# The 24 gate columns of an input projection as four float32 column groups of the array

## The chip, the cores and the metric

The kernel runs on one core of a Trainium2 chip. The metric is the device time of one execution in microseconds, as the median of several runs. Five engines matter here, each with an instruction stream of its own that it works off in order: TensorE (PE in the profile; PEld is its loading of weights), VectorE (DVE), ScalarE (ACT), GpSimd (POOL) and SyncE (SP), which issues most of the transfers.

## What is computed

One step of a decoder layer with 512 prompt tokens and 8 samples of 8 tokens, 576 tokens in all, of width 2048, in float32. The input is normalised, projected by w_in, and split into the inputs of eight gated-delta heads and four mLSTM heads. After these come an output projection, a convolutional feed-forward block and a final norm. What the change touches is the beginning:

```
h = _rmsnorm(x, norm_mix_g)
proj = jnp.einsum('bld,de->ble', h, w_in)
dn_qkv, dn_z, dn_b, dn_a, ml_q, ml_k, ml_v, ml_o, ml_i, ml_f = jnp.split(proj, idx, axis=-1)
...
beta = jax.nn.sigmoid(dn_b)
g = -jnp.exp(dn_A_log) * jax.nn.softplus(dn_a + dn_dt_bias)
...
ig = ml_i + ml_i_bias
logf = jax.nn.log_sigmoid(ml_f + ml_f_bias)
```

The four small pieces dn_b, dn_a (8 columns each), ml_i and ml_f (4 each) are the 24 gate columns. All other pieces are multiples of 128 columns wide. The norm is a factor 1/sqrt(mean of squares + eps) for each token, times norm_mix_g for each of the 2048 rows of w_in.

## The kernel before

The data lie transposed: features on the 128 partitions, 576 tokens along the free dimension. The input x is thus 16 tiles of 128 x 576 (k = 0 to 15). A float32 product is made of three products of a faster type, float32r: every operand is split into a high and a low part (`split`, lines 118 to 121: ScalarE casts, which is line 120, VectorE subtracts, which is line 121), and `three` (line 194 on) multiplies high by high, high by low and low by high. Each is done for two halves of 288 tokens, so one k of one 128-column tile is six matmuls, all at line 198. I call this a step. `dense` (line 201) makes one 128-column tile of a product in 16 steps: 96 matmuls. Its weights come in units of 128 x 1024 (eight k), loaded by SP's queue up to three units ahead (`load_unit`, `unit`); a unit's raw buffer, its high and its low part have two buffers each.

`startup` (lines 333 to 367) issues the loads of x, and after x 1 and x 3 those of the first two units. For every k, ScalarE and VectorE make the high part ah and the low part al of x times norm_mix_g (lines 356 and 357). The factor 1/sqrt isn't in them; it is multiplied in when a tile leaves PSUM. For it ScalarE squares all x (line 363), GpSimd adds up those of odd k and VectorE those of even k (line 365), and VectorE adds the two (line 366).

`gates` (line 370) sets up constants and then makes the first tile of w_in. In this tile, the host has put the 24 gate columns at columns 0, 32, 64 and 96, and zeros elsewhere; it costs as much as any tile of 128. Its two halves stay in two PSUM tiles pr (there are four pr of one bank, and two pd of two banks for the dense tiles). `gate_rows` (line 398) is a job: a generator that is advanced by `tick` after each step, and whose `yield n` lets n steps pass. This is how all the small work is spread between the dense steps; TensorE's order is that in which the program issues. Here the job waits for 14 steps after its first tick, then sums the squares over the partitions with a matrix of ones (`rms_bc`, whose two products are at line 256), forms rstd on ScalarE and VectorE (lines 244 to 248), multiplies the gates by it (line 406), waits 6 steps, and then works out the gates' functions in some 40 instructions, chiefly on VectorE. After twice 30 more steps it transposes the results, and only then can the job of the first head begin.

`mixer` (line 284) goes through the heads: for each of the eight delta heads the tiles q, k, v and z; the first three go to `conv_in` (line 518), which takes a tile out of PSUM times rstd (lines 528 to 530), and convolves it. A dense tile needs one of the two pd, so its first step waits until the tile before the last has been taken out. A head's job `dn_head` starts when its four tiles are there and the head before the last is done, the first head's when the gates are done.

On ScalarE, VectorE, GpSimd and in SP's queue the order is planned at build time from priorities and estimated durations; `urgent` raises a priority. The chip then keeps to that order.

Of the kernel before, what the change touches and what calls it, by code (L numbers as in the profile page):

```python
# [43 lines left out]
# columns of the parameter array  # L44
G1, G2, G3, CW, DG, MG, FW, FBI, GB, AL, M0, NPAR = 0, 16, 32, 48, 144, 145, 153, 417, 505, 506, 507, 515
# columns of the constant array
C_ID, C_INC, C_LV, C_IS, C_BM, C_SG, C_BD, C_RB, C_M3, NCON = 0, 128, 256, 640, 704, 712, 713, 841, 849, 853

# order of the 128-column tiles of w_in
# [19 lines left out]
class Layer:  # L69
# [25 lines left out]
    def open(self, name, **k):  # L95
        """A pool that close() ends (last in, first out on its side of the memory)."""
        stack = ExitStack()
        self.stacks[name] = stack
        return stack.enter_context(self.tc.tile_pool(name=name, **k))
# [48 lines left out]
    def plain_weights(self):  # L148
        for name, n in (("w_in", NIN), ("w_out", KT), ("w_up", 2 * NPL - 2)):
            for t in range(n):  # L150
                for u in range(2):
                    yield self.I[name][t][u], False
# [4 lines left out]
    def down_weights(self, b):  # L157
        """The weights of the plain blocks from b on, up to the next one of seven products."""
# [24 lines left out]
    def later(self, n, out, in_):  # L183
        """A store, queued n steps from now."""
# [16 lines left out]
    def dense(self, outs=None):  # L201
        """One 128-column tile of a K=2048 product."""
# [17 lines left out]
    def dense_pair(self):  # L220
        """Two tiles by turns, so that the first rows of the input are done with early."""
# [28 lines left out]
    def sum_bc(self, ss):  # L250
        """Sums over partitions of ss [P, NT], on all partitions."""
# [32 lines left out]
    def mixer(self):  # L284
# [5 lines left out]
        for h in range(DNH):  # L290
            q, k, v = (self.conv_in(8 * i + h, self.dense()) for i in range(3))
# [40 lines left out]
    def startup(self):  # L332
# [14 lines left out]
        acts = [self.new_act(k) for k in reversed(range(KT))][::-1]  # L347
        for k in range(KT):
            x = self.r()
            xs.append(x)  # L350
            nc.sync.dma_start(out=x, in_=I["xT"][k])
            if k in (1, 3):
                self.load_unit()
# [13 lines left out]
        self.acc = acc  # L367

# [1 line left out]
    def gates(self):  # L370
# [23 lines left out]
        outs = [self.psr()[:, 0:HALF] for _ in range(2)]  # L394
        self.dense(outs)
        return self.spawn(self.gate_rows(outs))

    def gate_rows(self, outs):
        nc, I, O = self.nc, self.I, self.O
        V, A, Pl = nc.vector, nc.scalar, nc.gpsimd  # L400
        yield 14
        self.rms_bc(self.acc[0], self.rstd)
        gr = self.r()
        for hf in range(2):
            sl = slice(hf * HALF, (hf + 1) * HALF)
            V.tensor_tensor(out=gr[:, sl], in0=outs[hf], in1=self.rstd[:, sl], op=ALU.mult)
        yield 6
# [10 lines left out]
        # softplus(y) = max(y, 0) + log1p(exp(-|y|)), log1p(e) = 2 atanh(e / (2 + e))  # L418
# [40 lines left out]
        # gated delta rows: log decay G, -exp(G), exp(Glast - G)  # L459
# [6 lines left out]
        # mLSTM rows (partitions 64-67)  # L466
# [51 lines left out]
    def conv_in(self, t, pd):  # L518
        """Depthwise convolution and silu of a projected tile."""
# [27 lines left out]
    def decay(self, bc, cols):  # L547
        """exp(min(bc_i - col_j, 0)) on and above the diagonal, else 0 (rows j, columns i)."""
# [20 lines left out]
    def lasts_of(self, bc):  # L569
        """The columns of bc at each chunk's last token."""  # L570
# [6 lines left out]
    def dn_head(self, h, q, k, v, sz):  # L577
# [14 lines left out]
        # natural k, norms of k  # L592
# [30 lines left out]
        # U = c_j (k_j . k_i) E, KQ = (k_j . q_i) E  # L623
# [19 lines left out]
        # v / |k| natural  # L643
# [18 lines left out]
        # chunk by chunk over the prompt  # L662
# [32 lines left out]
        # output norm; the scale of q only enters through the guard  # L695
# [10 lines left out]
    def pack(self, t, n, tag, order):  # L706
        """32 rows of t at a time as three groups of rows, each the high or the low parts."""
# [934 lines left out]
```

## Time and profile before

| what | value |
|---|---|
| median of 3 runs | 2703.66 us (2702.69 to 2705.25) |
| the profiled execution's span | 2704.9 us, granted TensorE clock 0.995 |
| the gate tile, first matmul to the next tile's first | 10.69 to 25.98 us |
| sums of squares over the partitions, first matmul | 41.77 us |
| bytes moved | 304.02 MB, mean 112 GB/s |

The profile is of one execution. A row of a timeline gives start, duration, engine, line, operation, the tile written and those read, the shape and the number of instructions merged; in brackets stands how long the engine was idle before, and what ended that. A row of waits gives the total, the number and the longest wait. A window row gives for each engine the busy time and the number of instructions, then the granted clock of TensorE, the transfers' share and rate. Matmuls overlap in TensorE's pipeline, so the spacing of their starts counts, not the duration of one.

### The profile page before, as it was taken

The numbers are of one execution on the slowest core, as the hardware profiler recorded it, in microseconds if no ns is written. First come the engines' busy times: TensorE is split into PE (matmuls) and PEld (weight loads), VectorE is DVE, ScalarE is ACT, GpSimd is POOL, SyncE is SP. The second block draws the span as 40 slices with busy tenths as digits, with TensorE's granted clock in tenths as the row PEclk, the third lists the DMA queues.
The fourth block names the chain that finished last, engine by engine and source line by source line (L and its number), as shares of the span: only waits on it lengthen the run. The fifth ranks groups of instructions, "written<-read, shape, count | busy, mean of one in ns | idle before, by whom it ended". The sixth has DMA issues, their size and how long they took to land.

```text
span 2704.9 us, 48701 instructions
## 1 busy us (share of the span) xinstructions
PE 2661.1 (98%) x19895; PEld 2620.4 (97%) x19895; DVE 1992.4 (74%) x3346; ACT 1072.4 (40%) x1694; POOL 327.8 (12%) x637
## 2 busy tenths in 40 slices
PE   7999999999999999998999999999999999999998
PEld 7999999999999999998999999999999999999998
DVE  7887777764444332289888888888888888988656
ACT  5334344433333232254444444444444443434324
POOL 2223222222111001111000000000000100000001
PEclk9999999999999999999999999999999999999999
DMA  5222222223332334444333333333333373342333
GB/s 195 85 79 92 91 83 91 91 88 105 112 107 89 122 127 134 137 124 149 107 107 107 109 111 110 107 107 107 107 107 107 107 255 99 105 145 71 121 96 100
DMA packets 112233, 304.02 MB, mean 112 GB/s; under 512 B 21912, under 2 KB 28184, under 8 KB 112008
## 3 DMA queue, kind: packets, MB, share of 16 engines
q1 hardware_dynamic: 107896, 291.17, 34.1%
q0 software_dynamic: 1872, 7.37, 0.8%
q8 instruction: 156, 2.56, 0.4%
q10 hardware_dynamic: 2240, 2.36, 0.3%
q14 instruction: 69, 0.57, 0.1%
HBM read 264.79 MB, written 36.06 MB: 111 GB/s over the span
## 4 chain that ended last, share of the span: by engine, by line
PE 88%; DVE 4%; DMA 1%; ACT 1%; issue 1%; POOL 0%; SPq 0%; DVEq 0%
PE pd L198 35%; PE pr L1265 31%; PE pd L1265 12%; PE pr L198 3%; PE pr L1491 1%; DMA r<-hid 1%; PE pr L991 1%; DVE wl L121 1%; PE pr L737 1%; DVE bl L121 0%; POOL irk L613 0%; DVE r L1526 0%; PE pr L832 0%; PE pr L256 0%; ACT r L603 0%
## 5 line engine op out<-in xcount | busy, mean ns | idle before, releaser
L120 ACT CAST wh<-raw 128x1024 fp32r<-128x1024 f32 (+1 forms) x394 | 404.6, 1027 | 744.7 <-PE pd L198 410.6
L1265 PE MATMUL pr<-bh,wh 128*128 128x288 f32 x2120 | 627.5, 296 | 2.2 <-ACT bh L120 2.2
L1265 PE MATMUL pr<-bl,wh 128*128 128x288 f32 x2120 | 625.0, 295 | 0.7 <-DVE bl L121 0.6
L1265 PE MATMUL pr<-bh,wl 128*128 128x288 f32 x2120 | 625.2, 295 | 0.1
L121 DVE TENSOR_TENSOR wl<-raw,wh 128x1024 fp32r<-128x1024 f32 (+1 forms) x394 | 474.4, 1204 | 183.3 <-ACT wh L120 177.0
L198 PE MATMUL pd<-ah,wh 128*128 128x288 f32 x2496 | 558.4, 305 | 0.0
L198 PE MATMUL pd<-ah,wl 128*128 128x288 f32 x2496 | 534.4, 296 | 0.0
L198 PE MATMUL pd<-al,wh 128*128 128x288 f32 x2496 | 534.2, 296 | 0.0
L198 PEld LDWEIGHTS pd<-ah,wh 128*128 128x128 f32 x2496 | 401.0, 189 | 9.5 <-issue 2.9
L198 PEld LDWEIGHTS pd<-ah,wl 128*128 128x128 f32 x2496 | 401.9, 189 | 0.0
L1265 PEld LDWEIGHTS pr<-bl,wh 128*128 128x128 f32 x2120 | 400.7, 189 | 1.1 <-DVE bl L121 1.1
L198 PEld LDWEIGHTS pd<-al,wh 128*128 128x128 f32 x2496 | 401.8, 189 | 0.0
L1265 PEld LDWEIGHTS pr<-bh,wh 128*128 128x128 f32 x2120 | 399.3, 188 | 2.4 <-ACT bh L120 2.4
L1265 PEld LDWEIGHTS pr<-bh,wl 128*128 128x128 f32 x2120 | 399.5, 188 | 0.8 <-DVE wl L121 0.8
L120 ACT CAST wh<-s 128x1024 fp32r<-128x1024 f32 (+1 forms) x171 | 169.5, 991 | 362.9 <-DVE s L1230 139.3
L1265 PE MATMUL pd<-bh,wh 128*128 128x288 f32 x848 | 252.0, 297 | 5.6 <-ACT wh L120 5.6
L1265 PE MATMUL pd<-bh,wl 128*128 128x288 f32 x848 | 250.9, 296 | 1.7 <-DVE wl L121 1.7
L1265 PE MATMUL pd<-bl,wh 128*128 128x288 f32 x848 | 249.9, 295 | 0.0
L121 DVE TENSOR_TENSOR wl<-s,wh 128x1024 fp32r<-128x1024 f32 (+1 forms) x171 | 196.5, 1149 | 27.0 <-ACT wh L120 19.6
L1265 PEld LDWEIGHTS pd<-bh,wh 128*128 128x128 f32 x848 | 160.2, 189 | 6.1 <-ACT wh L120 6.1
L1265 PEld LDWEIGHTS pd<-bh,wl 128*128 128x128 f32 x848 | 160.7, 189 | 2.3 <-DVE wl L121 2.3
L1265 PEld LDWEIGHTS pd<-bl,wh 128*128 128x128 f32 x848 | 160.9, 190 | 0.0
(391 smaller groups left out, 3514.1 us busy)
## 6 DMA issues: line engine op xcount, KB each, us to landing
raw<-in_w_up SPq DMA_DIRECT2D x176, 512.0 KB
raw<-in_w_in SPq DMA_DIRECT2D x114, 512.0 KB
raw<-in_w_down SPq DMA_DIRECT2D x40, 512.0 KB
raw<-in_w_out SPq DMA_DIRECT2D x32, 512.0 KB
raw<-in_w_down SPq DMA_DIRECT2D x40, 384.0 KB
hid<-r SPq DMA_DIRECT2D x44, 288.0 KB
r<-hid SPq DMA_DIRECT2D x40, 288.0 KB
r<-in_xT SPq DMA_DIRECT2D x32, 288.0 KB
```

What stands on the lines that cost most here:

```text
L120: nc.scalar.copy(hi, src)
L121: nc.vector.tensor_tensor(out=lo, in0=src, in1=hi.bitcast(F32), op=ALU.subtract)
L198: mm(outs[hf], w, x[:, hf * HALF:(hf + 1) * HALF], start=first and i == 0, stop=last and i == 2)
L737: mm(pr[:, 16 * b:16 * b + 16], st[:, b], kqs[:, b].rearrange("p a w -> p (a w)"), start=True, stop=True)
L991: mm(pn[0:64, 0:257], self.qim[:, b], caug[b // 4][:, b % 4], start=b == 0, stop=False)
L1265: mm(out, w[:, ks], x[:, sl], start=k == 0 and i == 0, stop=k == nk - 1 and i == 2)
L1491: mm(pr[:, 0:n], w[:, ks], acts[kk][:, a * NT + sl.start:a * NT + sl.stop], start=kk == 0 and i == 0, stop=kk == FB - 1 and i == 2)
```

## The change

The gate tile leaves the dense product. In `startup`, four loads of 128 x 512 (four k of the first tile of w_in each) go to SP's queue ahead of x 0, 4, 8 and 12, and GpSimd picks out 32 columns for each k, eight from each of the four places, and multiplies them by norm_mix_g (`gate_weights`). The first two units, now of tile q, are loaded after x 3 and x 7. The job `gate_rows` multiplies these weights with the raw x in float32: 16 k times two halves, 32 matmuls of 32 columns. Matmul k + j writes to partitions 32 j to 32 j + 31 of PSUM, so four k run in four column groups of the array and give four partial sums. It does four k at its first tick, which comes ahead of tile q's first step, and four more after steps 4, 8 and 12. ScalarE copies the partial sums to SBUF. GpSimd builds a matrix pick from the identity, and after the sums of squares, 14 steps later, a float32 product with pick adds the four groups and spreads the gates to the partitions 0, 32, 64 and 96 where the rest expects them. The gates' functions follow 8 steps later instead of 6. Of head 0, the tiles q and k are both issued before the first of them is taken out of PSUM. Everything else is the same; comments were dropped.

```diff
-        for name, n in (("w_in", NIN), ("w_out", KT), ("w_up", 2 * NPL - 2)):
-            for t in range(n):
+        for name, t0, n in (("w_in", 1, NIN), ("w_out", 0, KT), ("w_up", 0, 2 * NPL - 2)):
+            for t in range(t0, n):
...
-            q, k, v = (self.conv_in(8 * i + h, self.dense()) for i in range(3))
+            if h == 0:
+                self.tick()
+                pds = [self.dense(), self.dense()]
+                q, k = (self.conv_in(8 * i, pd) for i, pd in enumerate(pds))
+            else:
+                q, k = (self.conv_in(8 * i + h, self.dense()) for i in range(2))
+            v = self.conv_in(16 + h, self.dense())
...
+        self.gw = self.r(shape=[P, KT, 32])
         for k in range(KT):
+            if k % 4 == 0:
+                self.gate_weights(k)
             x = self.r()
             xs.append(x)
             nc.sync.dma_start(out=x, in_=I["xT"][k])
-            if k in (1, 3):
+            if k in (3, 7):
                 self.load_unit()
...
-        self.acc = acc
+        self.acc, self.xs = acc, xs
+
+    def gate_weights(self, k):
+
+        raw = self.r(shape=[P, 4, 4, 32])
+        self.nc.sync.dma_start(out=raw, in_=self.I["w_in"][0][k // 8][:, k % 8 * P:(k % 8 + 4) * P].rearrange("p (k g w) -> p k g w", k=4, g=4))
+        shape = [P, 4, 4, 8]
+        self.nc.gpsimd.tensor_tensor(out=self.gw[:, k:k + 4].rearrange("p k (g w) -> p k g w", g=4), in0=raw[:, :, :, 0:8],
+                                     in1=self.par[:, G1 + k:G1 + k + 4].unsqueeze(2).unsqueeze(3).to_broadcast(shape), op=ALU.mult)
...
-        outs = [self.psr()[:, 0:HALF] for _ in range(2)]
-        self.dense(outs)
-        return self.spawn(self.gate_rows(outs))
-
-    def gate_rows(self, outs):
+        return self.spawn(self.gate_rows())
+
+    def gate_rows(self):
         nc, I, O = self.nc, self.I, self.O
         V, A, Pl = nc.vector, nc.scalar, nc.gpsimd
+        halves = [slice(hf * HALF, (hf + 1) * HALF) for hf in range(2)]
+
+        outs = [self.psr()[:, 0:HALF] for _ in range(2)]
+        for k in range(0, KT, 4):
+            for out, sl in zip(outs, halves):
+                for j in range(4):
+                    nc.tensor.matmul(out[32 * j:32 * j + 32], self.gw[:, k + j], self.xs[k + j][:, sl], start=k == 0, stop=k == KT - 4)
+            if k < KT - 4:
+                yield 4
+        parts = self.r()
+        for out, sl in zip(outs, halves):
+            A.copy(parts[:, sl], out)
+
+        pick = self.r(shape=[P, 4, 32])
+        Pl.memset(pick, 0.0)
+        for j in range(4):
+            s = slice(32 * j, 32 * j + 32)
+            Pl.tensor_copy(pick[s, :, 0:8], self.ident[s, s].rearrange("p (g w) -> p g w", g=4))
         yield 14
         self.rms_bc(self.acc[0], self.rstd)
         gr = self.r()
-        for hf in range(2):
-            sl = slice(hf * HALF, (hf + 1) * HALF)
-            V.tensor_tensor(out=gr[:, sl], in0=outs[hf], in1=self.rstd[:, sl], op=ALU.mult)
-        yield 6
+        for sl in halves:
+            pr = self.psr()[:, 0:HALF]
+            nc.tensor.matmul(pr, pick.rearrange("p g w -> p (g w)"), parts[:, sl], start=True, stop=True)
+            V.tensor_tensor(out=gr[:, sl], in0=pr, in1=self.rstd[:, sl], op=ALU.mult)
+        yield 8
```

## The prediction

> **What bounds the kernel now.** I read the page first, then the waits of the first 110 us, then the first 75 us instruction by instruction, because everything that the diff touches lies there.
>
> ```profile
> span 2704.9 us, 48701 instructions
> PE 2661.1 (98%) x19895; PEld 2620.4 (97%) x19895; DVE 1992.4 (74%) x3346; ACT 1072.4 (40%) x1694; POOL 327.8 (12%) x637
> PE 88%; DVE 4%; DMA 1%; ACT 1%; issue 1%; POOL 0%; SPq 0%; DVEq 0%
> ```
> ```profile
> PE pr L198 <- ACT wh L120: 10.7, 1, 10.7
> PE pr L256 <- DVE r L366: 3.6, 1, 3.6
> ```
>
> TensorE is the bound: 98% busy, 88% of the chain that ended last. Work taken off it shortens the kernel as long as no new wait appears. Two of its waits are in the start: 10.7 us until the first weights are cast, and 3.6 us at line 256, where it is ready to sum the squares over the partitions but the squares are not yet added up. Since TensorE works in program order, that second wait holds up all dense products behind it.
>
> ```profile
> 10.69 0.85 PE L198 MATMUL pr<-ah,wh 128*128 128x288 f32 x2 [10.69 <-ACT wh L120]
> 15.24 0.55 PEld L198 LDWEIGHTS pr<-ah,wh 128*128 128x128 f32 x2
> 25.98 0.43 PE L198 MATMUL pd<-ah,wh 128*128 128x288 f32 x2
> 37.71 0.43 PE L198 MATMUL pd<-ah,wl 128*128 128x288 f32 x2
> 41.77 1.24 PE L256 MATMUL pr<-r,ones 128*128 128x288 f32 x4 [3.63 <-DVE r L366]
> 42.63 0.73 PE L198 MATMUL pd<-ah,wh 128*128 128x288 f32 x2
> 46.49 0.42 PE L198 MATMUL pd<-ah,wl 128*128 128x288 f32 x2
> 57.96 0.43 PE L198 MATMUL pd<-ah,wh 128*128 128x288 f32 x2
> ```
>
> The gate tile takes 10.69 to 25.98, 15.3 us. Tile q of head 0 follows. Between 25.98 and 37.71 stand 15 steps of k, that is 45 pairs of matmuls, so a pair takes 11.73 / 44 = 0.267 us and a step of three pairs 0.80 us. After step 15 the sums are due, and TensorE waits until 41.77. From 42.63 to 46.49 the eight pairs are at 0.48 us each, the half clock; so the wait of 3.6 us also costs 8 x (0.48 - 0.267) = 1.7 us behind it. Tile q's last step and the sixteen of tile k make 51 pairs, and tile v starts at 57.96. **That start of tile v is my yardstick**: whatever it moves by, the rest moves by, unless something later gives it back.
>
> **What is removed.** The 96 matmuls of the gate tile: 48 x 0.267 = 12.8 us of TensorE, or 15.3 us as they ran, with the slow start. ScalarE loses two casts, VectorE two subtractions of 1.2 us.
>
> ```profile
> L121 DVE TENSOR_TENSOR wl<-raw,wh 128x1024 fp32r<-128x1024 f32 (+1 forms) x394 | 474.4, 1204 | 183.3 <-ACT wh L120 177.0
> ```
>
> **What is added on TensorE.** 32 float32 matmuls of 288 columns, 32 of the array's 128 columns each. The nearest float32 rows, and the nearest stay in a narrower tile of the array:
>
> ```profile
> 650.98 3.69 PE L991 MATMUL pr<-st,qim 128*64 128x257 f32 x16
> 654.60 0.64 PE L992 MATMUL pr<-vas,r 64*64 64x257 f32 x2
> ```
> ```profile
> 163.18 0.42 PE L198 MATMUL pd<-ah,wl 128*128 128x288 f32 x2
> 163.53 0.68 PE L862 MATMUL pr<-r,r 128*64 128x64 f32 x8
> 164.14 0.53 PE L198 MATMUL pd<-ah,wh 128*128 128x288 f32 x2
> 164.51 0.42 PE L198 MATMUL pd<-al,wh 128*128 128x288 f32 x2
> ```
>
> Line 991 issues 8 products and the trace has 16 instructions: a float32 matmul is two. They take (654.60 - 650.98) / 16 = 0.226 us each, at 288 columns 0.226 x 288 / 257 = 0.253 us. The gates make 64 such instructions. One after another they cost 64 x 0.253 = 16.2 us; with the four groups side by side, a quarter, 4.0 us. No row shows two column groups at once, so these are the bounds. I take 8.1 us: in the diff the order is group 0, 1, 2, 3, both instructions of one matmul need the same columns and must follow each other, while the first of the next group can run beside the second. Each block of four k is then 2.0 us (bounds 1.0 and 4.0). Going to a narrower tile and back costs (163.53 - 163.18 - 0.133) + (164.51 - 164.14 - 0.267) = 0.3 us at most; with 0.2 us for each of the three blocks between dense steps, 0.6 us.
>
> The Trainium skill, page "TensorE: Matmul & The Clock Gate", section "Part 3: Packing small matmuls — row/col tiling", measured 2.38 times with three column groups; by that figure an estimate is 16.2 / 2.38 = 6.8 us, and no run here shows it. Its page "TensorEngine Tiling (Array Packing)", section "Key Properties", says that a change of tiling mode drains the array and a change of tile alone does not; the 0.3 us above agree with the first half, the second half is open here and would exclude the last of my rivals.
>
> Besides, two products with pick (four instructions of 0.253 = 1.0 us) stand behind the sums.
>
> **The start.** The first tick, ahead of the dense steps, issues the block of k 0 to 3, and the others come after steps 4, 8 and 12. The queue of SP now carries 256 KB of gate weights ahead of each four x, and the first weights of tile q behind x 3.
>
> ```profile
> GB/s 0 186 400 381 383 397 415 402 399 395 403 401 401 407 412 421 134 25 306 93 360 415 208 0 0 0 93 257 5 0 11 139 210 0 0 0 96 254 0 5
> q0 software_dynamic: 240, 1.03, 4.3%
> 9.60 1.04 ACT L120 CAST wh<-raw 128x1024 fp32r<-128x1024 f32 x1 [2.72 <-DMA raw<-in_w_in]
> 12.53 1.04 ACT L120 CAST wh<-raw 128x1024 fp32r<-128x1024 f32 x1 [0.23 <-DMA raw<-in_w_in]
> 13.48 6.51 ACT L356 ACTIVATE ah<-r,par 128x576 fp32r<-128x576 f32 x9
> ```
>
> From 3 us on the transfers run at 400 GB/s (slices of 1.5 us). The two weight units, landing at 9.6 and 12.5 us with 2.14 and 3.26 MB asked for by then (the 1.03 MB of the three loads on POOL's queue among them, an x being 0.295 and a unit 0.524 MB), fit 3 + (bytes - 0.28 MB) / 400 GB/s + 2 us, the 0.28 MB being those of the slice of 186 GB/s. By the same line the new order brings x 3 at 10.5, the first unit at 11.8 (cast at 12.9), x 7 at 15.4, x 11 at 20.3 and x 15 at 23.9 us. The blocks wait for x 3, 7, 11 and 15, each due before its step. Dense steps then start at 13.1 instead of the gate tile's 10.69. The array is slow for its first 4.6 us as in before (10.69 to 15.24), of which about 1.1 us are left to lose. TensorE stands at the sums after 26 steps: 13.1 + 26 x 0.80 + 1.1 + 3 x (2.0 + 0.2) = 41.6 us (38.6 with full overlap; one after another, with the first block lasting until 15.1, 15.1 + 20.8 + 0.6 + 12.7 = 49.2).
>
> **When the squares are added up.**
>
> ```profile
> 25.39 1.82 POOL L365 TENSOR_TENSOR r<-r,r 128x576 f32<-128x576 f32 x1 [18.28 <-ACT r L363]
> 28.27 11.97 POOL L365 TENSOR_TENSOR r<-r,r 128x576 f32<-128x576 f32 x6 [1.05 <-ACT r L363]
> 36.54 2.45 DVE L121 TENSOR_TENSOR wl<-raw,wh 128x1024 fp32r<-128x1024 f32 x1
> 38.91 1.95 DVE L365 TENSOR_TENSOR r<-r,r 128x576 f32<-128x576 f32 x1
> 40.96 0.76 DVE L366 TENSOR_TENSOR r<-r,r 128x576 f32<-128x576 f32 x1
> 5.50 0.47 POOL L379 TENSOR_SCALAR cwh<-par 128x96 f32<-128x96 f32 x1 [2.49 <-DMA par<-in_par]
> 50.22 0.21 POOL L532 COPY dnst<-r 128x27 f32<-128x27 f32 x1 [9.30 <-DVE r L530]
> ```
>
> GpSimd's seven additions, from 25.39 to 40.24, set this time, with VectorE's last two behind. In before ScalarE paced them (nine ah in 6.51 us, without a gap). Now x 15 comes at 23.9 instead of 21.3 (6.80 MB by the same line), 2.6 us later, but ScalarE gets gaps for squares meanwhile, and the fourth square, which lets GpSimd begin, should be there at 25 us as before. GpSimd's four multiplications of gate weights (0.47 us each by line 379) lie in its 18 us of idleness before 25.39; without that cover they cost 1.9 us. The memset and four small copies for pick (0.2 us each, line 532, some 0.8 us in all) can fall among the additions. The two copies of the gates' sums (0.50 us each, by line 244 below) fall in ScalarE's idleness before 42 us; they are new on its queue, and a square placed behind them would wait for the block of k 12 to 15. So the squares are added up at 41.77 + 0.7 = 42.5 us. They could be there at 41, if the subtraction of 36.54 (2.45 us beside GpSimd's additions) no longer stands ahead of VectorE's last addition, and as late as 45, if the squares come later by all of the 2.6 us of x 15.
>
> The sums then run at 42.5, and the wait shrinks from 3.6 us to 0.9; I count no half clock behind it (it would cost up to the 1.7 us above). The multiplications by rstd:
>
> ```profile
> 42.56 0.50 ACT L244 ACTIVATE rstd<-pr,eps 128x288 f32<-128x288 f32 x1 [6.44 <-PE pr L256]
> 43.88 1.04 ACT L120 CAST wh<-raw 128x1024 fp32r<-128x1024 f32 x1 [0.82 <-PE pd L198]
> 44.83 0.49 ACT L244 ACTIVATE rstd<-pr,eps 128x288 f32<-128x288 f32 x1
> 49.88 0.21 DVE L530 TENSOR_TENSOR r<-pd,rstd 128x64 f32<-128x64 f32 x1
> ```
>
> Tile v needs q's PSUM tile back (there are two pd), and in before that was 50.09 - 41.77 = 8.3 us after the sums began. TensorE's own work to tile v is sums 1.0 + pick 1.0 + 6 steps 4.8 = 6.8 us. So a new short wait of up to 1.5 us stands there; 1.8 us of the 8.3 came from a cast queued between the two halves on ScalarE (43.0 to 44.83) and may go. I take the full 8.3: tile v starts at 42.5 + 8.3 = 50.8 instead of 57.96. **Sum: 7.2 us gained.** The span of 2704.9 becomes 2697.7; it stands 1.2 us above the median of 2703.66, inside the three runs' 2702.69 to 2705.25, so the median becomes 2696.5. The best case is 41 + 6.8 = 47.8, a gain of 10.2.
>
> Later: the gate rows end after step 103 of the dense stream instead of 91 (by the yields), so heads 0 and 2 run 12 steps later; head 2 ends at step 312, and head 4 can't start before its own tiles at 320. The shift ends there.
>
> **The rivals.** (1) The four groups run one after another: sums at 49.2, tile v at 49.2 + 8.3 = 57.5, time 2703.2, no change. For it: no row of this trace shows two groups at once. (2) VectorE gives it back.
>
> ```profile
> 60.00:70.00 10.00, 10.00 (x77) 10.00 (x77) 9.77 (x14) 1.05 (x1) 0.94 (x3) 1.00 0.36 107
> 100.00:110.00 10.00, 10.00 (x79) 10.00 (x79) 6.52 (x16) 3.31 (x7) 4.52 (x4) 1.00 0.34 105
> 110.00:120.00 10.00, 10.00 (x80) 9.73 (x80) 5.69 (x13) 5.57 (x21) 2.37 (x2) 1.00 0.25 84
> ```
>
> VectorE (third figure in busy time) is full from 60 us and has 3.5 + 4.3 = 7.8 us free in 100 to 120. Dense tiles that come 7.2 us earlier need that and the 2.4 us of subtractions saved. If its order, which is fixed beforehand, lets only the 3.5 us of the first of these windows be used, 7.2 - 3.5 = 3.7 us go: 2700.2, within 0.2%. Against it: TensorE is busy for all 10 us of each of these windows. (3) Slower: each instruction of a column group waits until the one ahead has left the array: 0.41 us, which is what one of line 256 takes from its start to its end, instead of 0.253.
>
> ```profile
> L256 PE MATMUL pr<-r,ones x4: 406/406/510, 41.8 to 42.6; 128*128 128x288 f32 x4
> ```
>
> Blocks are then 6.5 us, the sums at 16 (the first block) + 21.1 + 3 x 6.7 = 57.2, tile v at 65.5, a loss of 7.5: 2711.2. It decides from 0.26 us an instruction on, and from 0.37 us it passes 0.2%.
>
> **Chances.** Forecast 0.60, rival 1 0.18, rival 2 0.15, rival 3 0.07. About 0.2%, 5.4 us, is what a measurement of this kernel tells from no change. With the squares at 45 the forecast's gain is 57.96 - 53.3 = 4.7 us, below that, and I give this end 1 in 8 of its 0.60; a fifth of rival 2 stays above it. Faster 0.56, same 0.37, slower 0.07. The range goes from the best case, 2693.5, to rival 1, 2703.2; the rest lies outside. The forecast alone: 2693.5 to 2699.0.
>
> **What would show it.** In the profile after: the gates' 64 instructions in four blocks, the later three about 2.0 us apiece between dense steps (4.0: rival 1; 6.5: rival 3); the wait before line 256's counterpart under 1.5 us, with no half clock behind it; the sums near 42.5 and tile v near 50.8; no new wait of TensorE between 60 and 140 us (rival 2). The forecast is wrong if the first dense step starts after 15 us, or if the squares are added up after 45.

## The result, and the profile after

| | old kernel | changed kernel |
|---|---|---|
| median of 4 runs each | 2704.10 us (2702.69 to 2705.25) | 2718.79 us (2716.86 to 2720.78) |
| ratio, 95% interval | | 1.0052 [1.0039, 1.0064] |
| span of the profiled execution | 2704.9 us | 2715.1 us |
| start of tile v of head 0 | 57.96 us | 51.02 us |

The changed kernel is slower by 0.5%, some 14 us by the medians. Between the two profiled executions it is 10.2 us. The one of the changed kernel is the fastest of its four runs; its time is 1.8 us above its span, and by the same step the old kernel's execution would stand at some 2706.7 us (an estimate), above its four runs. So the spans show less than the medians. Lines from 292 on have moved by up to 34: a line n of the heads' jobs before is n + 34 after.

The page of the changed kernel opens as that of the old one did:

```profile
span 2715.1 us, 48668 instructions
PE 2657.3 (98%) x19867; PEld 2611.6 (96%) x19867; DVE 1999.1 (74%) x3344; ACT 1071.8 (39%) x1694; POOL 333.7 (12%) x646
```

TensorE's busy time fell by 3.8 us, and the span grew by 10.2. So 14.0 us of idleness came in, and the shares of the span cannot show where. The start does not hold them; this is TensorE's timeline of the changed kernel up to tile v:

```profile
10.24 4.25 PE L422 MATMUL pr<-r,r 128*32 128x288 f32 x16 [10.24 <-DMA r<-in_xT]
14.42 0.85 PE L198 MATMUL pd<-ah,wh 128*128 128x288 f32 x2
...
18.33 1.18 PE L422 MATMUL pr<-r,r 128*32 128x288 f32 x16
19.43 0.53 PE L198 MATMUL pd<-ah,wh 128*128 128x288 f32 x2
...
22.81 1.18 PE L422 MATMUL pr<-r,r 128*32 128x288 f32 x16
...
27.30 1.18 PE L422 MATMUL pr<-r,r 128*32 128x288 f32 x16
...
42.50 1.89 PE L256 MATMUL pr<-r,ones 128*128 128x288 f32 x4 [2.64 <-DVE r L375]
44.18 2.12 PE L439 MATMUL pr<-r,r 128*128 128x288 f32 x4
45.69 0.96 PE L198 MATMUL pd<-ah,wh 128*128 128x288 f32 x2
...
51.02 0.42 PE L198 MATMUL pd<-ah,wh 128*128 128x288 f32 x2
```

The gates stand in four blocks (line 422), the sums of squares (256) begin at 42.50, and tile v at 51.02: a gain of 6.9 us, where 7.2 was forecast. What follows shows in the list of waits of the changed kernel (line waited for: total, number, longest, in us):

```profile
PE pr L866 <- issue: 12.1, 2, 11.3
PE pr L422 <- DMA r<-in_xT: 10.2, 1, 10.2
...
PE pd L198 <- DVE r L301: 4.1, 1, 4.1
PE pr L688 <- POOL r L814: 2.9, 1, 2.9
PE pr L256 <- DVE r L375: 2.6, 1, 2.6
```

The two long ones, 11.3 us at line 866 and 4.1 us at a dense step, are new, and so are the 2.9 us at line 688. The places of the first two in the timeline of the changed kernel:

```profile
93.67 0.49 PE L198 MATMUL pd<-ah,wh 128*128 128x288 f32 x2 [4.09 <-DVE r L301]
...
290.52 2.05 PE L866 MATMUL pr<-r,r 128*128 128x128 f32 x8 [11.33 <-issue]
...
293.32 0.68 PE L198 MATMUL pd<-ah,wl 128*128 128x288 f32 x2
293.80 0.68 PE L198 MATMUL pd<-ah,wh 128*128 128x288 f32 x2
```

Behind the second, pairs are 0.48 us apart instead of 0.267: the half clock again. The windows of the two stretches show the same in the seventh figure, the granted clock. The changed kernel:

```profile
80.00:100.00 20.00, 15.91 (x109) 15.70 (x109) 19.43 (x38) 8.49 (x14) 0.82 (x3) 0.91 0.25 81
280.00:300.00 20.00, 9.48 (x57) 9.51 (x58) 8.35 (x24) 3.90 (x5) 0.00 (x0) 0.66 0.18 45
```

and the old one:

```profile
80.00:100.00 20.00, 20.00 (x153) 20.00 (x153) 19.80 (x41) 10.27 (x16) 2.62 (x6) 1.00 0.27 83
280.00:300.00 20.00, 20.00 (x163) 19.27 (x162) 6.57 (x16) 8.11 (x28) 3.19 (x4) 1.00 0.30 96
```

A clock to read the loss by is ScalarE's cast of each weight unit (line 120): cast i of the changed kernel against cast i + 2 of the old one, which has two units more. The difference is -7.0 us from 50 to 80 us, -3.7 at 102, about 0 from 180 to 205, +2.7 at 263, +12.6 at 306, and between +10.6 and +12.7 from there to 1400 us. So all of it is lost between 83 and 306 us, a good part of it at the two waits. (Where a head's own matmuls come earlier or later in the dense stream, the casts move too, without a loss; they measure it where the heads are in step again, as they are from 369 us on.)

**What TensorE waits for at 290 us.** Line 866 needs T, the inverse of head 2's diagonal blocks. It is made in a chain (`inverse`): VectorE folds the blocks into cb (lines 821 and 822), SP sends them to DRAM and back as u, VectorE substitutes in 28 small instructions (838 and 840), SP sends x out and back as cx, and VectorE expands it (857) and transposes it (859). TensorE meanwhile does 29 steps. I measure the chain from the last transposition of v (line 654, after: 688) to the end of line 859 (before: 825), and the cover from the same start to where TensorE stands ready for T:

```
                 head 0       head 1       head 2       head 3      heads 4-6
                 chain cover  chain cover  chain cover  chain cover chain cover (us)
old kernel       27.4  27.5   25.7  30.3   28.3  26.9   29.1  27.8  26.2  26.9
changed kernel   34.5  33.9   27.6  29.7   35.7  24.5   27.1  29.8  26.2  26.9
```

In the old kernel, too, this chain had hardly any cover to spare (waits of 1.45 and 1.54 us at heads 2 and 3). In the changed one head 2 has 7.4 us more chain and 2.4 us less cover. VectorE's timeline of the changed kernel shows what stands between two links of head 2's chain, the folding and the writing of cb:

```profile
258.58 0.29 DVE L821 TENSOR_TENSOR r<-r 128x128 f32<-128x128 f32 x1
258.79 0.45 DVE L562 TENSOR_TENSOR r<-pd,rstd 128x288 f32<-128x288 f32 x1
259.16 0.38 DVE L563 TENSOR_TENSOR r<-pd,rstd 128x224 f32<-128x224 f32 x1
259.45 0.21 DVE L564 TENSOR_TENSOR r<-pd,rstd 128x64 f32<-128x64 f32 x1
259.59 1.21 DVE L121 TENSOR_TENSOR wl<-raw,wh 128x1024 fp32r<-128x1024 f32 x1
260.72 0.23 DVE L822 TENSOR_TENSOR cb<-r 128x64 f32<-128x64 f32 x1
```

Taking the next tile out of PSUM (562 to 564) and a weight unit's low part (121) come in between, and so it goes on: from the chain's start to the end of cb it takes 6.2 us against 3.8 before, from there to the substitution 7.5 against 5.9, and the substitution, from 268.44 to 284.56, 16.1 against 13.5. The view marks no gap of VectorE from 255.7 to 284.6.

### The profile page after: what moved, and what is told of

Read it like the earlier page. It is cut to its first block, busy times and chain, and to the rows that moved or that the text cites. A ratio compares the mean times of both kernels' runs of the same rounds, so it can differ in the third digit from the quotient of the medians.

```text
span 2715.1 us, 48668 instructions
## 1 busy us (share of the span) xinstructions
PE 2657.3 (98%) x19867; PEld 2611.6 (96%) x19867; DVE 1999.1 (74%) x3344; ACT 1071.8 (39%) x1694; POOL 333.7 (12%) x646
## 3 DMA queue, kind: packets, MB, share of 16 engines
q8 instruction: 156, 2.56, 0.4%
## 4 chain that ended last, share of the span: by engine, by line
PE 89%; DVE 6%; DMA 2%; issue 1%; ACT 1%; POOL 0%; SPq 0%; DVEq 0%; ACTq 0%; POOLq 0%
PE pd L198 36%; PE pr L1299 31%; PE pd L1299 12%; PE pr L198 3%; PE pr L1525 1%; DVE wl L121 1%; DVE bl L121 1%; PE pr L1025 1%; PE pr L771 0%; DMA r<-hid 0%; DMA r<-in_xT 0%; PE pr L256 0%; POOL irk L647 0%; DVE r L374 0%; DVE r L1560 0%
```

## The experiments

Times are medians, ratios against the old kernel's runs on the same chip; "the casts" is the comparison above. In the kernels made from the changed one, head 0 begins at step 103 of the dense stream, unless something else is said.

| kernel | us | ratio, 95% interval |
|---|---|---|
| changed, both pauses 24 instead of 30 | 2716.42 | 1.0047 [1.0032, 1.0062] |
| old, both pauses 36 | 2720.05 | 1.0057 [1.0040, 1.0073] |
| changed, z tile of head 0 by ScalarE | 2715.11 | 1.0041 [1.0026, 1.0056] |
| changed, pauses 24 and z by ScalarE | 2718.32 | 1.0053 [1.0038, 1.0068] |
| changed, 14 steps more for head 2 | 2719.43 | 1.0053 [1.0040, 1.0066] |
| old, pauses 36 and 14 steps more | 2716.42 | 1.0043 [1.0031, 1.0056] |
| **z early** (changed, VectorE takes z out early) | 2713.54 | 1.0032 [1.0020, 1.0044] |
| z early, 14 steps more | 2713.37 | 1.0035 [1.0023, 1.0048] |
| z early, 14, 3 and 2 steps more at heads 2, 4, 5 | 2719.24 | 1.0051 [1.0039, 1.0064] |
| z early, low parts by GpSimd | 2718.40 | 1.0050 [1.0036, 1.0063] |
| z early, head 2 free | 2705.98 | 1.0003 [0.9995, 1.0012] |
| z early, head 2 free, 5 steps more | 2706.11 | 1.0001 [0.9992, 1.0010] |
| changed, head 2 free, 5 steps more | 2711.98 | 1.0026 [1.0015, 1.0036] |
| old, head 2 free, 5 steps more | 2703.41 | 0.9994 [0.9985, 1.0003] |
| z early, free, 5 more, head 0 at 99 | 2707.47 | 1.0010 [1.0002, 1.0019] |
| the same, head 0 at 91, short series | 2704.52 | 1.0001 [0.9992, 1.0010] |
| old, free, 5 more, short series | 2704.15 | 0.9999 [0.9990, 1.0007] |

### Is it only where head 0 stands?

Head 0 begins 12 steps later than in the old kernel. The first pair of runs moves only that, in both directions.

```diff
-        yield 30        # both, changed kernel
+        yield 24
```

> The changed kernel with the two waits of 30 steps between the parts of the gate rows cut to 24, so that the transposes of the gates and head 0 begin at step 82 and 91 of the dense stream, as before the change. Theory A (alignment): the change won its 7 us by 50 us and lost some 20 us later in two places, 4.1 us (5.9 with the half clock behind it) where tile k of head 1 waits for the PSUM tile of z of head 0, and 11.3 us (13 with the half clock) where the inverse of head 2 waits at line 866, because heads 0 and 2 run 12 steps later than before. Then this kernel has no wait of over 3 us at line 866 before 320 us, and its time is 2718.8 - 13 = 2706 (2703 to 2709). Theory R (VectorE is full): VectorE can't follow tiles that come 7 us earlier, and gives the time back as a wait wherever the heads stand. Then waits of 10 us and more show up elsewhere between 90 and 320 us, and the time stays at 2715 or more.

```diff
-        yield 30        # both, old kernel
+        yield 36
```

> The kernel before, with the two waits of 30 steps in the gate rows made 36: nothing but head 0's begin moves, from step 91 to 103 of the stream of tiles behind the gate tile. Theory A: the wait of head 2's inverse (line 832 here) comes up without the change, 8 to 12 us with a half clock behind it, and the time is 2704 + 10 to 14, some 2715. Theory R: the tiles come no earlier than in the kernel before, so VectorE follows: within 3 us of 2704.

The old kernel with head 0 put back by 12 steps loses 15.7 us, and the list of waits shows why:

```profile
PE pr L832 <- issue: 11.2, 2, 10.3
```

Line 832 is its line 866: 10.3 us for head 2's T, a chain of 34.7 us against a cover of 24.4. The delay alone makes this wait and a loss of the same size, with none of the gate products moved. But bringing head 0 back to step 91 does not undo it; the changed kernel with the short pauses still waits in the same places:

```profile
PE pr L866 <- DVE r L859: 11.5, 2, 8.7
PE pd L198 <- DVE r L301: 3.1, 1, 3.1
```

Head 2 then starts at 242.3 us instead of 254.7, but its chain still takes 34.8 us (cover 26.2), and head 3 waits too (31.0 against 28.5). So my first theory, that the place in steps is what counts, is half of it at most.

### The z tile of head 0

```profile
89.47 1.16 DVE L508 TENSOR_TENSOR_SCAN r<-r,par,r 4x8 f32<-4x8 f32 x8
92.07 0.68 DVE L523 TENSOR_TENSOR r<-r,mp 4x512 f32<-4x512 f32 x1
92.77 0.76 DVE L301 SCALAR_TENSOR_TENSOR r<-pd,rstd 128x576 f32<-128x576 f32 x1
```

These rows are VectorE's in the changed kernel. The z tile is taken out of its PSUM tile at 92.77 (line 301), behind the gates' rows (508, 523), although TensorE had finished it at about 77 us. The old kernel did it at 93.01, where its TensorE, 7 us behind, did not need the tile yet. So the dense stream came earlier and VectorE did not. In the first attempt ScalarE copied the tile out (with priority); it went into ScalarE's order hardly earlier, at 91.70 us:

```diff
+            zp = self.halves(pd)
+            if h == 0:
+                zt = self.r()
+                zp = self.v2(zt)
+                with self.urgent():
+                    A.copy(zp, self.halves(pd))
...
```

> The changed kernel, but tile z of head 0 is copied out of PSUM by ScalarE (one copy of 128 x 576, at raised priority), and VectorE multiplies the copy later; so its PSUM tile is free without VectorE. Theory A: the wait of 4.1 us at line 198 near 90 us goes, with the half clock behind it, the wait of 11.3 us at line 866 stays: 2718.8 - 5.9 = 2713. Theory R: the wait goes from this place, but the time comes back as longer waits at heads 0 to 2: 2717 to 2720.

> The gate rows' waits of 24 steps and ScalarE's copy of tile z together, on the changed kernel. Theory A: both places mended, the gain of the start is left: 2704 - 7 = 2697, at most 2701. Theory R: 2710 or more, with the time in other waits between 90 and 320 us.

The wait fell to 2.6 us in both, the one for head 2 stayed at 11.1 and 8.7 us: the theory missed both times. In the second attempt the third part of the gates' rows is tied behind the z tile:

```diff
-                V.scalar_tensor_tensor(out=self.v2(sz), ...)
+                self.last_evac = V.scalar_tensor_tensor(out=self.v2(sz), ...)
...
-        yield 30        # then 30
+        yield 33        # then 27
```

> The changed kernel, in which VectorE takes the z tile of head 0 out of PSUM ahead of the third part of the gates' rows (the part is tied behind that instruction, and comes 3 steps later; the transposes after it come at the same step as before). Theory: the wait of tile k of head 1 for this PSUM tile (4.1 us, and about 1.8 us of half clock behind it) is gone, the weights' casts at 110 us are then 5 to 7 us ahead of the old kernel's; what becomes of head 2 is open, since each new order of VectorE has moved that wait: between 2700 (no wait there) and 2714 (its 11.3 us stay). Rival (the gates' rows are late themselves: what this moves behind the z tile delays the transposes and head 0 by as much): the casts at 110 us are no more than 3 us ahead, and a wait of 3 us or more stands at the gates' transposes or at head 0's first products.

The wait is gone, and the window of 80 to 100 us is full again:

```profile
80.00:100.00 20.00, 20.00 (x152) 20.00 (x152) 19.27 (x37) 9.77 (x16) 0.82 (x3) 1.00 0.25 81
```

The casts are 7.9 us ahead at 112 us (3.8 in the changed kernel), and the time is 5.3 us less than the changed kernel's 2718.79 (by the two ratios, which differ by 0.0020, 5.4 us). The 11.2 us at line 866 stay. The z tile's share of the loss is thereby shown.

### More steps for head 2's inverse

```diff
-        inv = self.inverse(U, res, YZ if h == 0 else 0)
+        inv = self.inverse(U, res, YZ if h == 0 else 14 if h == 2 else 0)
```

> The changed kernel, in which only the inverse of head 2 is given 14 steps more (43 instead of 29) before TensorE asks for its T. Theory (what the changed kernel loses is the 11.3 us for which TensorE waits at L866 for head 2's T, and about 1.7 us of half clock behind it, because the chain of 35.7 us has only 29 steps, some 27 us, of cover): the wait is gone, and the time falls by about 12 us, from 2717 to 2705 (2702 to 2709). Rival (VectorE and SyncE are full in this stretch, and a wait bought off here comes back at a later head or at a tile's PSUM): the wait is smaller at head 2, but others of together 8 us or more stand behind it, and the time stays at 2713 or over.

> Both edits together on the changed kernel: the z tile of head 0 taken out ahead of the third part of the gates' rows, and 14 steps more for the inverse of head 2. Theory: the two losses are separate, and the sum of both is gained, 6 and 13 us: about 2698 (2694 to 2704), which is faster than the old kernel by the 7 us of its start. Rival (VectorE full): 2708 or over, with waits of another name of together 8 us or more before 400 us.

> The old kernel with both pauses of the gates 36 steps long instead of 30 (which gave 2720 us and a wait of 10.3 us for head 2's T), and with 14 steps more for the inverse of head 2. Theory (the cover of head 2's inverse is the one thing that the delay broke): the wait is gone and the time comes back to about 2706 (2703 to 2709). Rival (the delay of head 0 costs by itself, because VectorE then has more to do in less time): 2713 or over, with waits elsewhere.

All three times are the rival's, though in the first two the other waits come to less than the 8 us that it forecast. The waits of the first of them:

```profile
PE pr L866 <- DVE r L859: 4.3, 2, 2.5
PE pr L866 <- issue: 3.8, 2, 3.1
```

At head 2, 11.3 us became 3.1. But its end, 14 steps later, puts back head 4, which may begin only when head 2 is done; heads 4 and 5 then have chains of 29.3 and 29.4 us against covers of 26.8 and 27.8 and wait 2.5 and 1.8 us, with a half clock (0.91 in this window of the same kernel):

```profile
400.00:420.00 20.00, 17.52 (x119) 17.08 (x118) 16.86 (x38) 7.07 (x9) 6.93 (x10) 0.91 0.23 72
```

The casts go from +1.1 us at 294 to +12.3 at 497. The two waits, and the half clock behind the waits at 294 and 415 us (3.4 us each time, so 1.7 us lost), make some 8 us of that; the rest was not taken apart, and head 2's own matmuls, put off by 14 steps, are in it. I then bought off each of these waits in turn:

```diff
-        inv = self.inverse(U, res, YZ if h == 0 else 0)
+        inv = self.inverse(U, res, {0: YZ, 2: 14, 4: 3, 5: 2}.get(h, 0))
-PR = 0
+PR = 1000
```

> The changed kernel with the z tile taken out early and steps added to the inverses: 14 for head 2, 3 for head 4, 2 for head 5, and T is expanded at a higher priority on VectorE (with the 14 steps alone the wait at head 2 was still 3.1 us, because VectorE took the expansion behind an operation of head 3 that waited for a DMA, and heads 4 and 5, put back by head 2, waited 2.6 and 2.0). Theory (each wait is a chain of some 29 us against too few steps, and nothing else is lost): all three are under 0.8, and with the half clock behind each the time falls from 2713.4 to 2702 (2698 to 2706). Rival (whatever cover is given, the next head is put back and waits in turn): waits of together 4 us or more at other heads, 2709 or over.

A miss, and in the rival's way: head 2 waits 2.2 us, and head 4, whose chain grew to 33.7 us, now 4.5. In these kernels, cover that puts a head's end later is paid for by the head after the next.

### What makes the chain long, VectorE's other work or head 2's place?

```diff
-        nc.vector.tensor_tensor(out=lo, ...)
+        (nc.gpsimd if 30 <= self.ns <= 36 else nc.vector).tensor_tensor(out=lo, ...)
```

> The changed kernel with the z tile of head 0 taken out early, in which the low parts of the weights' blocks 30 to 36, those beside head 2's inverse, are worked out by GpSimd instead of VectorE (four of 1.21 us each stood between the links of the chain). Theory (the chain is long because VectorE's other work stands between its links): it falls by 3 to 5 us from 35.5, the wait from 11.2 to 6 to 8, the time from 2713.5 to 2709 (2706 to 2712). Rival (the chain's length is DMA latency and the queue, not VectorE): chain and wait as they were, within 1 us.

Here `self.ns` counts the splits. This run tells little, because the edit brought a cost of its own: the chain is 38.1 us, and TensorE waits for GpSimd's low parts.

```profile
PE pr L866 <- DVE r L859: 8.2, 1, 8.2
PE pd L198 <- POOL wl L121: 2.5, 1, 2.5
```

The other edit leaves VectorE's work alone and changes head 2's place. Heads 4 to 6 begin right behind their z tiles; head 2 has to wait for head 0, and so begins about a tile later beside the dense stream.

```diff
-            jobs.append(self.spawn(self.dn_head(h, q, k, v, sz), [jobs[0]] + jobs[-2:-1]))
+            jobs.append(self.spawn(self.dn_head(h, q, k, v, sz), [jobs[0]] + (jobs[-2:-1] if h != 2 else [])))
```

> The changed kernel with the z tile of head 0 taken out early (2713.5 us, head 2's T waited for 11.2 us), in which head 2 no longer waits until head 0 is done, so that it begins right behind its own z tile, where heads 4 to 6 begin too. Theory (head 0 begins 12 steps later than in the old kernel, because the gates' rows on VectorE end no earlier, so head 2, which waits for head 0, begins about a tile later beside the dense stream, and its inverse falls on VectorE's work for the next heads' q, k and v): the chain of head 2's inverse falls from 35.5 to 26 to 29 us, the wait from 11.2 to 2 or less, and the time to 2700 (2697 to 2705). Rival (the chain is long because VectorE has too much to do at this time whatever head 2's place): chain 32 or over, wait 6 or over, 2708 or over.

```profile
PE pr L866 <- DVE r L859: 4.1, 1, 4.1
```

7.6 us less, by an edit that takes no work away: head 2's place is the larger part of what z early still lost against the old kernel. Its inverse begins at 231.4 us instead of 251.1; a dense tile with the work in it takes some 17. The chain is 32.6 us against a cover of 28.5. That is the rival's length (32 or over; the theory had 26 to 29), while the wait of 4.1 us and the time lie between the two.

> The changed kernel with the z tile of head 0 taken out early and head 2 free of head 0 (2706 us, where head 2's T was still waited for 4.1 us: a chain of 32.6 us against 28.5), and with 5 steps more for the inverse of head 2. Head 4 began 8 us later beside head 2 than heads 5 and 6 beside theirs, so it should not be put back. Theory (place and cover of head 2's inverse are all that the changed kernel lost behind the z tile): the wait is 0.5 or less, the half clock behind it is gone, and the time falls by 4 to 7 us to 2700 (2697 to 2704), under the old kernel's 2705. Rival (the 7 us of the start cannot be kept, whatever is freed, since the gates' rows and head 0 on VectorE end no earlier): a wait of 3 us or more stands elsewhere before 400 us, and the time is 2704 or over.

> The changed kernel with head 2 free of head 0 and 5 steps more for its inverse, its z tile of head 0 taken out late as it was. Theory (two separate losses): the wait of 4.1 us for the z tile's PSUM and its half clock stay, head 2's wait of 11.3 is 1 or less: 2706 (2702 to 2709), some 5 us over the kernel that has the z tile early too. Rival (the edits hang together, as other orders of VectorE did): a wait of 4 us or more at head 2, 2711 or over.

> The old kernel with the same two edits of head 2 (free of head 0, 5 steps more). It tells whether the change is worth its 7 us of start where both kernels have head 2 free. Theory (the old kernel's own loss at heads 2 and 3 was waits of 1.45 and 1.54 us): they go, and the time is 2701 to 2705, that is 2 to 5 us over the changed kernel with all three edits. Rival (head 2 ahead of its old place meets head 0's last work on VectorE): waits of 3 us or more at head 2, and 2706 or over.

(The added edit is `YZ if h in (0, 2) else 0`.) With 5 steps more, head 2 waits no longer (chain 31.8, cover 31.9), and this time head 4 is not put back, but the median stays: 2706.11 (the profiled execution, with 2703.34, is one of the fastest of eleven). TensorE's remaining waits in this kernel are small ones:

```profile
PE pr L688 <- POOL r L814: 4.0, 2, 2.8
PE pr L889 <- DVE r L880: 2.6, 1, 2.6
PE pr L866 <- DVE r L859: 1.9, 1, 1.9
PE pr L789 <- ACT r L722: 1.7, 1, 1.7
```

The casts are 8.3 us ahead at 97 us, 6.2 at 162, 4.4 at 219 and 2.1 at 275. That is the rival of this run, though no wait reaches its 3 us: the lead melts, and the waits stand where heads begin and at their inverses. Without the early z tile the same edits give 2711.98, 5.9 us more, so the two losses are separate, as expected (the time itself was expected at 2702 to 2709). And the old kernel with head 2 free is at 2703.41: its waits of 1.45 and 1.54 us went down to nothing and 0.2 us, and by the medians it is 2.7 us below the changed kernel with all edits, where 2 to 5 above was expected, though the two intervals overlap. In it head 2's chain takes 26.1 us, from 233.9 us on; in the changed kernel with all edits it takes 31.8 from 230.9. So head 2's place is not all that makes the chain long. What else does, VectorE's order or head 0's work 12 steps later beside it, was not separated. No version of the changed kernel beat the old one by what can be measured.

### Why the rest of the lead is lost

My next theory was that VectorE, full from 60 to 98 us, ends the gates' rows no earlier in time, so that head 0 falls 7 us later in TensorE's work. In the next two kernels the series of the gates is cut short:

```diff
-        for c in (15, 13, 11, 9, 7, 5, 3):
+        for c in ():
...
-        yield 27        # changed kernel alone: head 0 at step 91
+        yield 15
```

> The changed kernel with all three edits (z tile early, head 2 free, 5 steps more for its inverse: 2706 us), in which the seven multiply-adds of the gates' series on VectorE (7 times 0.74 us) are left out, so that the gates are wrong, and head 0 begins at step 91 of the dense stream as in the old kernel, instead of 100. Theory (the 7 us of the start cannot be kept because VectorE, full from 60 to 98 us, ends the gates' rows no earlier, so that head 0 falls 7 us later in TensorE's work and closer to head 1): with 5.2 us less on VectorE head 0 keeps its old place, and the time is 4 to 7 us below the old kernel with the same edits and the same instructions left out, at 2695 to 2699. Rival (the loss between 110 and 240 us has another cause): 2703 or over, less than 2 us below that kernel.

> The old kernel with the two edits of head 2 (2703.4 us), with the same seven multiply-adds left out, so that the gates are wrong, and nothing else. It is what the run above is compared with. Theory: VectorE's relief does not reach TensorE here, since head 0's place is fixed by steps: 2703 (2700 to 2706). Rival (VectorE's load at the start costs the old kernel time as well): 2699 or under.

The theory fell. (Head 0 stood at step 103 in the kernel before, not at 100.) Head 0 is back in its old place with its old chain (27.3 us), and the two kernels are level, 2704.52 against 2704.15. The lead of 7.7 us at 112 is 3.7 at 132 and gone at 246; the longest waits are again where heads begin:

```profile
PE pr L688 <- DVE r L654: 5.0, 2, 2.6
PE pr L866 <- DVE r L859: 1.8, 1, 1.8
PE pr L889 <- DVE r L880: 1.1, 1, 1.1
```

> The changed kernel with all three edits (2706 us), in which head 0 begins 4 steps earlier, at step 99, which is about where the gates' rows are ready (98.4 us). Theory (each step that head 0 comes earlier gives it more room to head 1): 1 to 4 us less, 2702 to 2705. Rival (place is not what counts, or the rows are late): a wait at the gates' transposes or at head 0 takes its place, and the time is 2706 or over.

A miss as well: 2707.47, with waits of 3.1 us at head 0's T and 2.9 at head 2's. Head 0's place is not what eats the last 6 us between 110 and 250 us. Where they go can be read from the trace of the kernel with head 0 at 91: TensorE waits 2.4 us at 117.8, 1.1 at 158.7 and 2.6 at 233.8, and behind the first and the third the clock is at 0.50 for 3.4 us, which loses 1.7 us each time. That makes 9.5 us, enough for the whole lead. What stays open is what would shorten these waits. That VectorE and the short chains through four engines at each head's start can't go faster is likely, but it was only argued: nothing was run that takes them away.

### How the column groups run

```diff
-                    nc.tensor.matmul(out[32 * j:32 * j + 32], ...)
+                    nc.tensor.matmul(out[0:32], ...)
...
```

> The changed kernel, in which all sixteen products of a gate block go to the first group of 32 columns instead of four groups in turn (the one sum then takes all 16 rows of x; the picking matrix reads that group alone). If the four groups of columns work at the same time, a block that took 1.1 us takes 4 us (16 products of 0.25 us), and the dense stream begins about 9 to 12 us later in the three later blocks and the first together. If they do not, and the 1.1 us have another reason (short products after one another), the block stays at 1.1 us.

The second block of this kernel:

```profile
19.54 4.07 PE L422 MATMUL pr<-r,r 128*32 128x288 f32 x16
23.54 0.53 PE L198 MATMUL pd<-ah,wh 128*128 128x288 f32 x2
```

4.00 us from its start to the next step's, against 1.10 us with four groups (18.33 to 19.43): 0.25 us for each of the 16 instructions, and 0.069. The four groups do work at the same time, 3.6 times as fast as one. That kernel took 2722.72 us in its one run.

## Why the prediction was wrong

**The start, right.** The first dense step came at 14.42 instead of 13.1, the later blocks took 1.1 us instead of 2.0, the squares were added up at 42.5 as forecast, and tile v began at 51.02 instead of 50.8. That it came out so near is in part luck, since some sizes made up for each other. No half clock had been counted behind the sums, but there was one: sums and pick took from 42.50 to 45.69, 3.2 us instead of 2.0. The wait of up to 1.5 us for q's PSUM tile did not come.

**The gate blocks, mis-sized.** The term was 2.0 us, chosen between 1.0 and 4.0 because both instructions of a float32 product would have to follow each other. They do not hinder the other groups: 1.1 us, next to the lower bound. The Trainium skill, page "TensorE: Matmul & The Clock Gate", section "Part 3: Packing small matmuls — row/col tiling", gave 2.38 times with three groups; the trace has 3.6 times with four. It changed nothing in the end, since TensorE waited 2.64 us at the sums anyway. Rivals 1 and 3, in which the groups don't overlap, are thereby out.

**The step that failed:** "heads 0 and 2 run 12 steps later; head 2 ends at step 312, and head 4 can't start before its own tiles at 320. The shift ends there." The steps were counted rightly: head 4 did begin in its usual place. But the shift was priced at nothing, for no reason other than that it ended. No row was looked up for what heads 0 and 2 do while they are late. One stood in the old kernel's waits:

```profile
PE pr L832 <- DVE r L825: 3.0, 2, 1.5
```

TensorE already waited for T at heads 2 and 3, so any longer chain or shorter cover there would show at full price. It cost 11.3 us and the half clock behind it. The old kernel with the same delay of 12 steps waits 10.3 us in this place and loses 15.7 in all.

**The second step that failed** is the forecast's reason against rival 2, "TensorE is busy for all 10 us of each of these windows". That tells that VectorE did not hold TensorE up then, not that it would not when TensorE comes 7 us earlier. VectorE was full from 60 to 100 us (39.4 us busy of 40 in the old kernel) and took the z tile out at 92.77, as it had at 93.01. This is rival 2's mechanism (its fixed order does not follow), with 4.1 us of wait and a half clock; I gave it 0.15, and priced its whole loss at 3.7 us by free VectorE time alone, without asking which instruction would be late for whom.

**What was not in the list at all** is a slower kernel by way of a later stage. The only rival on that side lay in the gate products.

## What to carry to other kernels

A gain at the start is worth what the stages behind it let through: ask for each job that the change moves against the main stream which wait of that job is near zero now, and what comes to stand beside it, and price the move by the half clock too. A wait of 1.5 us on a chain of VectorE's work and a round trip through DRAM on either side of the substitution is a warning, not a trifle. Buying cover by putting an end later moves the wait to whoever waits for that end; moving the beginning to where the other heads begin was the edit that helped.

## What the runs showed of the hardware

Four column groups of 32 overlap almost wholly in float32: 16 instructions of 288 columns in 1.10 us, against 4.00 us in one group.

A short wait can halve the clock, and one as long can leave it alone, because the clock is decided in fixed stretches of 3.41 us. In the changed kernel it is at half from 42.94, 94.14 and 281.87 us on, for 3.41, 3.41 and 13.65 us; these lengths and the distances between the starts are whole multiples of 3.41 us, and so it is in every trace of this case up to 2600 us. What counts is how long TensorE idles within one such stretch. In the changed kernel the 2.64 us at the sums fell into one stretch, and the next was at 0.50 (second figure: TensorE's busy time; seventh: the clock):

```profile
39.53:42.94 3.41, 0.77 (x5) 0.48 (x4) 3.20 (x4) 0.85 (x1) 3.33 (x4) 1.00 0.27 109
42.94:46.35 3.41, 3.41 (x10) 2.28 (x9) 2.46 (x5) 1.00 (x2) 1.23 (x4) 0.50 0.50 150
```

In the kernel with z early, head 2 free and 5 steps more, TensorE waited 2.56 us at line 889, from 270.4 to 273.0 us. The boundary at 272.00 parted the wait, and the clock stayed:

```profile
268.59:272.00 3.41, 1.84 (x14) 1.61 (x13) 3.41 (x5) 0.00 (x0) 1.91 (x2) 1.00 0.38 102
272.00:275.41 3.41, 2.42 (x22) 2.38 (x23) 2.54 (x5) 1.38 (x4) 0.00 (x0) 1.00 0.34 138
275.41:278.82 3.41, 3.41 (x30) 3.17 (x29) 3.00 (x7) 0.89 (x1) 0.00 (x0) 1.00 0.11 14
```

The 2.86 us at line 688 of the changed kernel, ending at 156.55, were parted in the same way. Counted by the profiles' busy times over the 20 traces, from their first half clock to 2600 us, each of the 87 stretches in which TensorE idled for 1.92 us or more was followed by one at half clock, and no stretch at full clock with less than 1.59 us was; between these, 7 of 20 were.

The Trainium skill's page "TensorE: Matmul & The Clock Gate", section "Part 1: The HAM clock gate (the "warmup" mystery)", speaks of an idle window of about 3.4 us that runs freely. The traces agree on the window and its free run, but it need not be idle as a whole: 1.92 us of its 3.41 were enough.
